# Layer 0's feed-forward: half of its pairs of up tiles as seven block products in place of eight

## The chip, the cores and the metric

The kernel runs on one core of a Trainium2 chip. A core has a matrix engine (TensorE, PE in the profile, with its weight loads as PEld), VectorE (DVE), ScalarE (ACT), GpSimd (POOL) and SyncE (SP), which mostly issues DMAs here. Each engine works through its own list of instructions in order; semaphores between the lists make one wait for another. The metric is the device time of one execution in microseconds (us); lower is better. Times given are medians of several executions; the profile is of one execution.

## The reference

Two blocks of a network follow each other, all in 32-bit floats. The first maps 256 tokens of width 1024 through one gated linear attention layer and a squared-ReLU MLP. The second has two layers over 256 latent and 256 context tokens. Layer 0 mixes by neighbourhood attention, layer 1 by grouped-query attention, and each has a SwiGLU feed-forward (FFN) with a hidden width of 2816. Scale, shift and gate of every norm and residual come from a conditioning vector by one matrix product a layer (`ada`), six rows of 1024 for each layer, for the latent and for the context tokens.

```
def swiglu_ffn(h, w_in, w_out):
    a, g = jnp.split(h @ w_in, 2, axis=-1)
    return (jax.nn.silu(a) * g) @ w_out

def ada_norm(x, g, shift, scale):
    return rms_norm_2(x, g) * (1.0 + scale) + shift
```

In layer 0, latent and context tokens pass through the same FFN weights, so its up product is 512 tokens x 1024 by 1024 x 5632, and its down product 512 x 2816 by 2816 x 1024.

## The kernel before, in words

**Products.** All large products are made in three terms. A weight tile `raw` of 128 x 1024 comes from DRAM (`w_load`, SP). `w_split` turns it into a high part `wh` (a cast on ACT, line 178) and a low part `wl` (a subtraction on DVE, line 179), and the activations are split the same way. `mm3` (lines 193 to 195) adds high x high, low x high and high x low in a PSUM bank. Weight tiles are used in the order of one long list, `UNITS`; `wnext` takes the next and loads and splits some ahead.

**Layer 0's FFN.** The hidden width is 22 tiles of 128; a *pair* is the tile of `a` and the tile of `g` for the same hidden columns. `ffn_up` makes a pair: for each of its two weight tiles eight steps over the input width, three products each, with 512 tokens as moving columns, 48 products of 128x512 in all. `ffn_act` (lines 1109 to 1119) evacuates it: silu on ACT, the product with `g` on DVE (line 1112), a cast on ACT, a subtraction on DVE (line 1119). The first two pairs are made in halves of 256 tokens (`ffn_up_first`). The 22 pairs go in two halves of 11. After each half, `ffn_down0` makes the down product in PSUM banks, which `gated` multiplies by the gate and adds to the residual (lines 1080 and 1081). After the second half the context tokens' down products come first, and the normalising and transposing of the context tokens for layer 1 (`to_T`, lines 232 to 251) is put inside the last call for the latent tokens. The key and value products of layer 1 (`kv_pass`) come next.

**The conditioning steps.** `ada_jobs` makes the rows of `ada` without PE: for eight slices of each row it loads 128 x 1024 numbers (512 KB, SP, line 304, two buffers of tag `ada`) and lets DVE multiply them by the conditioning vector and sum them (line 324, one pass for a *single* step; two for a *double* one, which serves latent and context). After eight steps POOL adds a bias (line 339), and for gate rows PE transposes the result (line 348) so that it can be written to DRAM and fetched again spread over the partitions (`load_gates`). Steps are taken from a generator by `ada_run`. `adaC` has 24 double and 32 single steps; the FFN takes two of them beside each pair and one beside each down tile.

**Order.** A scheduler at build time lays every engine's instructions into one list from the program's dependences and its own estimates, so the program's text sets the order only in part; the lists quoted below are those of the built kernels.

Of the kernel before, what the change touches and what calls it, by code (L numbers as in the profile page):

```python
# [17 lines left out]
P = 128  # L18
# [10 lines left out]
HALF = NFT // 2  # L29
# [7 lines left out]
def _units():  # L37
# [23 lines left out]
    for part in range(2):  # L61
        for f in range(part * HALF, (part + 1) * HALF):
            u += [("f", "ffn_in0", P * f), ("f", "ffn_in0", FH + P * f)]
        dn = [("h", "ffn_out0", part * HALF + f, 512 * h) for h in range(2) for f in range(0, HALF, 2)]
        u += dn if part == 0 else dn + dn
# [18 lines left out]
def net(ctx, tc, x, xt, small, gk_up, gk_b, g_onorm, wst, final_norm, ctx_in, ctx_t, ada, ada_b, cvec,  # L84
# [76 lines left out]
    def w_split(upto):  # L161
        while wpos[1] < min(upto, len(UNITS)):
            i = wpos[1]
            raw = raws.pop(i)
            n = 512 if UNITS[i][0] == "h" and UNITS[i][1] == "ffn_out0" and (UNITS[i][2] % HALF) == HALF - 1 else 1024
# [14 lines left out]

    def wnext(kind):
# [10 lines left out]
    def mm3(o, lh, ll, rh, rl, first, last):  # L192
        T.matmul(o, lhsT=lh, rhs=rh, start=first, stop=False)  # L193
        T.matmul(o, lhsT=ll, rhs=rh, start=False, stop=False)  # L194
        T.matmul(o, lhsT=lh, rhs=rl, start=False, stop=last)  # L195
# [30 lines left out]
    def to_T_steps(xns, dst, t0, scale=None, bias=None):  # L226

        n = P * len(xns)
        for k in range(KD):
# [12 lines left out]
            else:  # L242
                r = t2([n])
# [33 lines left out]
    def mm_h(o, u, j, xp, t, first, last):  # L277
        h, l = u
        c = slice(j * 512, (j + 1) * 512)
        mm3(o, xp[0][:, t * P:(t + 1) * P], xp[1][:, t * P:(t + 1) * P], h[:, c], l[:, c], first, last)  # L280
# [93 lines left out]
    adaC = ada_jobs([(0, 5, True), (1, 0, True), (1, 1, True)] + [(1, v, False) for v in (3, 4, 2, 5)])  # L374
# [726 lines left out]
    fT = new_T2()  # L1101
    o_half(1, 2, hc, 1)
    xn = [normed(t) for t in hc]
    o_half(0, 0, lat, 0)
    o_half(1, 0, lat, 0, lambda: to_T(xn, fT, S, mod(0, 1, 4), mod(0, 1, 3)))
# [16 lines left out]
    def ffn_up(L, src, n):  # L1122
        ps_ = []
        for _ in range(2):
            u = wnext(("f", f"ffn_in{L}"))
            o = bank()
            for k in range(KD):
                mm_f(o[:, :n], u, src, k, 0, n, k == 0, k == KD - 1)
            ps_.append(o)
        return ffn_act(*ps_, n)  # L1130

    def ffn_up_first(src):

        us, os_ = [], []
        for _ in range(4):
            us.append(wnext(("f", "ffn_in0")))
            os_.append(bank())
            for k in range(KD):
                mm_f(os_[-1][:, S:N2], us[-1], src, k, S, S, k == 0, k == KD - 1)
        to_T(xn, src, 0, mod(0, 0, 4), mod(0, 0, 3))  # L1140
        z = []
        for n in range(4):
            for k in range(KD):
                mm_f(os_[n][:, 0:S], us[n], src, k, 0, S, k == 0, k == KD - 1)
# [4 lines left out]
    def ffn_down0(hf, uu, tiles, between=None):  # L1149
        ac = {t: bank() for t in tiles}  # L1150
        for f2 in range(0, HALF, 2):
            u = wnext(("h", "ffn_out0"))
            for j in range(min(2, HALF - f2)):
                f = f2 + j
                for t in tiles:
                    mm_h(ac[t], u, j, uu[f], t, f == 0, f == HALF - 1)
            ada_run(adaC)
            if f2 == 4 and between is not None:
                between()
        for t in tiles:  # L1160
            gated((lat + hc)[t], ac[t], 0, t // 2, 5, hf)
# [19 lines left out]
    for part in range(2):  # L1181
        uu = []
        for f in range(HALF):
            if part == 0 and f < 2:
                uu += ffn_up_first(fT) if f == 0 else []
            else:
                uu.append(ffn_up(0, fT, N2))
            ada_run(adaC, 2)
        if part == 0:
            load_gates(0, 5)  # L1190
            for hf in range(2):
                ffn_down0(hf, uu, (2, 3, 0, 1))
        else:
            for hf in range(2):
                ffn_down0(hf, uu, (2, 3))
            xn = [normed(t) for t in hc]
            ffn_down0(0, uu, (0, 1))
# [3 lines left out]
            ffn_down0(1, uu, (0, 1), lambda: to_T(xn, bT2, S, mod(1, 1, 1), mod(1, 1, 0)))  # L1201
# [310 lines left out]
    load_gates(1, 5)  # L1512
# [186 lines left out]
```

## Time and profile before

| | before |
|---|---|
| median of 3 runs | 1257.45 us (1257.27 to 1258.41) |
| the profiled execution, its own time | 1256.72 us |
| its span in the trace | 1254.9 us |
| PE busy | 1244.0 us, 99% |
| DVE busy | 919.9 us, 73% |
| ACT busy | 688.2 us, 55% |
| ada passes on DVE (line 324) from 570 to 870 us | 80 passes, 96.5 us |
| last ada pass starts at | 802.2 us |

The span is what the trace covers; the execution's own time is 1.8 us longer. Busy times count an engine's arithmetic, not its waits. A row of the timeline gives the start, the duration, the engine, the line of the source, the operation, and what it writes and reads, with buffer numbers left out.

### The profile page before, as it was taken

The page shows a single profiled execution, that of the slowest core. Times are in us where ns is not written, and L with a number is a line of the kernel's source. Part 1 is how long each engine was busy: PE and PEld are TensorE (multiplying, and loading weights), DVE is VectorE, ACT ScalarE, POOL GpSimd, SP SyncE. Part 2 cuts the span into 40 slices and gives each one's busy share as a digit, 9 for nine tenths or more (in the row PEclk, how much of TensorE's full clock was granted, in tenths as well). Part 3 has the DMA queues.
Part 4 walks back from the last instruction along what each step waited for, and adds up shares of the span by engine and source line. Part 5 has one row for each costly group of instructions (what it writes and reads, how often), then busy time and mean ns, then how long its engine had stood idle before and what let it go on. Part 6 is the DMA issues. An engine that isn't in the chain of part 4 may idle for free.

```text
span 1254.9 us, 18667 instructions
## 1 busy us (share of the span) xinstructions
PE 1244.0 (99%) x6872; PEld 1043.2 (83%) x6872; DVE 919.9 (73%) x1638; ACT 688.2 (55%) x1344; POOL 78.7 (6%) x137
## 2 busy tenths in 40 slices
PE   9999999999999999999999999999999999999997
PEld 8888889898888777789888888887888777999997
DVE  6959888697989887777877767633667988655555
ACT  8575655666549888655232222323456897544443
POOL 1010000030100000001000000000003220000000
PEclk9999999999999999999999999999999999999999
DMA  8647687787673333463656877633662324656650
GB/s 304 189 151 237 192 289 268 271 277 246 198 249 111 105 110 118 160 197 118 213 177 206 259 266 249 205 100 102 197 204 76 113 84 131 219 187 185 186 185 34
DMA packets 68507, 231.22 MB, mean 184 GB/s; under 512 B 8048, under 2 KB 8736, under 8 KB 68416
## 3 DMA queue, kind: packets, MB, share of 16 engines
q1 hardware_dynamic: 68128, 229.68, 57.0%
q8 instruction: 54, 0.88, 0.3%
q10 hardware_dynamic: 288, 0.35, 0.1%
q14 instruction: 37, 0.30, 0.1%
HBM read 228.93 MB, written 1.07 MB: 183 GB/s over the span
## 4 chain that ended last, share of the span: by engine, by line
PE 95%; ACT 2%; DVE 1%; issue 1%; DMA 0%; POOL 0%; SPq 0%; POOLq 0%; ACTq 0%
PE b L193 28%; PE b L194 28%; PE b L195 28%; PE b L1000 2%; PE b L1469 1%; PE b L981 1%; PE b L232 1%; PE b L1455 1%; PE b L562 1%; PE b L962 1%; PE b L963 1%; PE b L951 1%; PE b L1436 1%; DVE wl L179 0%; DMA t<-in_xt_dram 0%
## 5 line engine op out<-in xcount | busy, mean ns | idle before, releaser
L178 ACT CAST wh<-raw 128x1024 fp32r<-128x1024 f32 (+1 forms) x308 | 320.7, 1045 | 392.8 <-PE b L194 292.4
L179 DVE TENSOR_TENSOR wl<-raw,wh 128x1024 fp32r<-128x1024 f32 (+1 forms) x308 | 372.5, 1216 | 154.9 <-ACT wh L178 151.9
L193 PE MATMUL b<-t,wh 128*128 128x256 f32 (+1 forms) x1120 | 365.7, 327 | 0.0
L194 PE MATMUL b<-t,wl 128*128 128x256 f32 (+1 forms) x1120 | 365.6, 327 | 0.0
L195 PE MATMUL b<-t,wh 128*128 128x256 f32 (+1 forms) x1120 | 365.3, 327 | 0.0
L193 PE MATMUL b<-wh,t 128*128 128x512 f32 (+1 forms) x748 | 299.2, 402 | 1.2 <-ACT t L250 0.6
L194 PE MATMUL b<-wh,t 128*128 128x512 f32 (+1 forms) x748 | 294.8, 394 | 0.0
L195 PE MATMUL b<-wl,t 128*128 128x512 f32 (+1 forms) x748 | 294.7, 394 | 0.0
L193 PEld LDWEIGHTS b<-t,wh 128*128 128x128 f32 x1120 | 210.7, 188 | 22.2
L194 PEld LDWEIGHTS b<-t,wl 128*128 128x128 f32 x1120 | 210.8, 188 | 21.9
L195 PEld LDWEIGHTS b<-t,wh 128*128 128x128 f32 x1120 | 210.5, 188 | 20.4 <-DVE t L251 0.2
L195 PEld LDWEIGHTS b<-wl,t 128*128 128x128 f32 x748 | 140.4, 188 | 34.2
L193 PEld LDWEIGHTS b<-wh,t 128*128 128x128 f32 x748 | 140.4, 188 | 32.2 <-ACT t L250 1.0
L194 PEld LDWEIGHTS b<-wh,t 128*128 128x128 f32 x748 | 140.8, 188 | 30.1 <-DVE t L251 0.5
L324 DVE CUSTOM_DVE_ANT_0 a<-a,crow 128x1024 f32<-128x1024 f32 x96 | 117.6, 1233 | 28.8 <-DMA a<-in_ada_dram 28.3
L324 DVE CUSTOM_DVE_ANT_0 t<-a,crow 128x1024 bf16<-128x1024 f32 x64 | 78.5, 1237 | 7.3 <-DMA a<-in_ada_dram 7.1
L1112 DVE TENSOR_TENSOR t<-b,t 128x512 f32<-128x512 f32 (+1 forms) x42 | 23.7, 564 | 59.4 <-PE b L195 52.2
L205 POOL TENSOR_TENSOR c<-c,mhalf 128x1 f32<-128x1 f32 x21 | 14.2, 676 | 539.0 <-DVE c L204 538.9
L339 POOL TENSOR_TENSOR mod<-mod,bcol 128x8 f32<-128x8 f32 x20 | 13.4, 671 | 475.1 <-DVE mod L324 472.7
L1118 ACT CAST t<-t 128x512 fp32r<-128x512 f32 (+1 forms) x42 | 21.7, 516 | 28.6 <-DVE t L1112 28.6
L212 ACT ACTIVATE t<-t 128x512 f32<-128x512 f32 x40 | 24.8, 624 | 10.8 <-DVE t L1081 6.4
L1445 ACT ACTIVATE t<-b,c,c 128x512 f32<-128x512 f32 x32 | 26.0, 812 | 3.5 <-POOL c L1443 3.5
(244 smaller groups left out, 1212.6 us busy)
## 6 DMA issues: line engine op xcount, KB each, us to landing
raw<-in_wst_dram SPq DMA_DIRECT2D x310, 512.0 KB, 4.4
a<-in_ada_dram SPq DMA_DIRECT2D x96, 512.0 KB, 4.4
t<-in_rpb_dram SPq DMA_DIRECT2D x16, 256.0 KB, 4.5
t<-row SPq DMA_DIRECT2D x12, 256.0 KB, 5.1
t<-in_ctx_dram SPq DMA_DIRECT2D x8, 256.0 KB, 5.6
t<-in_xt_dram SPq DMA_DIRECT2D x4, 256.0 KB, 5.8
t<-in_x_dram SPq DMA_DIRECT2D x4, 256.0 KB, 6.5
crow<-in_cvec_dram SPq DMA_DIRECT2D x2, 512.0 KB
```

Source lines behind the costliest of these rows:

```text
L178: A.copy(out=h[:, :n], in_=raw[:, :n])
L179: V.tensor_tensor(out=l[:, :n], in0=raw[:, :n], in1=h[:, :n], op=ALU.subtract)
L193: T.matmul(o, lhsT=lh, rhs=rh, start=first, stop=False)
L194: T.matmul(o, lhsT=ll, rhs=rh, start=False, stop=False)
L195: T.matmul(o, lhsT=lh, rhs=rl, start=False, stop=last)
L205: G.tensor_tensor(out=ms[:, 3:4], in0=ms[:, 2:3], in1=mhalf[:, 0:1], op=ALU.pow)
L212: A.activation(out=junk[hf], in_=halves[hf], func=AF.Square, scale=1.0 / 32.0, accum_out=ms[:, hf:hf + 1])
L324: V.tensor_tensor_reduce(out=raw if ci == n_c - 1 else t2([D], BF16), in0=raw, in1=crow[ci], scale=1.0, scalar=0.0, op0=ALU.mult, op1=ALU.add,
L1000: T.matmul(po[e * 64:(e + 1) * 64, cols_], lhsT=v, rhs=probs[(head, "l" if lat_q else "c")][:, c, :], start=(c == 0), stop=(c == n_c - 1))
L1112: V.tensor_tensor(out=a, in0=pg_[:, :n], in1=a, op=ALU.mult)
L1118: A.copy(out=h, in_=a)
L1445: A.activation(out=pl, in_=sl, func=AF.Exp, scale=r, bias=mx[:, 1:2], accum_out=mx[:, 2:3])
```

## The change

- **Four parts for two halves.** The 22 pairs go in parts of 6, 6, 6 and 4. After each part the down product goes on accumulating: `ffn_down0` copies the four banks to SBUF (`dsum`) for one half of the output columns and copies the other half's sums back into the banks (`seed`), and products then accumulate onto them. `ffn_down0_last` does the last part, context first, then latent, with `gated` at its end.
- **Seven block products.** For 11 of the pairs, those listed in `SEVEN`, the pair is taken as a 2 x 2 block product: the two weight tiles by the two halves of the input width, and the two halves of the input by latent and context tokens. Seven products of block sums replace the eight plain ones (`ffn_up7`). Each is 12 products of 128x256, 84 a pair.
- **What the sums need.** `pair_sums` makes the weight sums on DVE and splits three full tiles and a half one, beside the pair before. `token_sums` makes the sums of the tokens once, after pairs 2 to 4, from unsplit copies `fX`. The banks of `ffn_up7` are copied out by ACT and summed by DVE in between (lines 1237 to 1262).
- **Residuals.** The residual tiles are written to DRAM after pair 2 (`put_away`) and read back in the last part (`fetch`).
- **Conditioning steps.** `adaC` has 48 steps (24 double, 24 single). One is taken beside each pair (none beside pair 3) one after the third part and one beside six of the last part's down tiles; what is left is taken in one call, `ada_run(adaC, 100)`, ahead of the last down call. The eight steps of row (1, 5) are a generator of their own, `adaD`, taken beside the first 12 hidden tiles of layer 1's FFN.

Line numbers move: 179 becomes 180, 193 to 195 become 198 to 200, 232 becomes 237, 324 becomes 329, 348 becomes 353, 1080 becomes 1086.

```
-HALF = NFT // 2
+PARTS = ((0, 6), (6, 12), (12, 18), (18, 22))
+SEVEN = (5, 7, 9, 11, 13, 14, 16, 17, 19, 20, 21)
...
-        while wpos[1] < len(UNITS) and wpos[1] - wpos[2] + 1 < cap[0]:
+        while wpos[1] < len(UNITS) and wpos[1] - wpos[2] + 1 < cap[0] and not seven(UNITS[wpos[1]]):
...
-    adaC = ada_jobs([(0, 5, True), (1, 0, True), (1, 1, True)] + [(1, v, False) for v in (3, 4, 2, 5)])
+    adaC = ada_jobs([(0, 5, True), (1, 0, True), (1, 1, True)] + [(1, v, False) for v in (3, 4, 2)])
+    adaD = ada_jobs([(1, 5, False)])
...
+    def ffn_up7(got, conv):
+        wpos[2] += 2
+        r, q, g = [bank()[:, 0:S] for _ in range(3)]
+        c1, c2, c3 = t2([2, S]), t2([2, S]), t2([2, S])
+        H = KD // 2
+
+        def prod(o, n, c, X, first=True):
+            h, l = got[n]
+            for j in range(H):
+                k = slice(c + j * P, c + (j + 1) * P)
+                mm3(o, h[:, k], l[:, k], *X(j), first and j == 0, j == H - 1, not first)
...
+        prod(r, 0, 0, lambda j: a(0, j))
+        A.copy(out=c1[:, 0, :], in_=r)
+        prod(q, 1, 0, lambda j: sT[(3, j)])
+        A.copy(out=c3[:, 0, :], in_=q)
+        run(conv)
+        prod(r, 2, 512, lambda j: sT[(2, j)], False)
+        A.copy(out=c3[:, 1, :], in_=r)
+        prod(g, 0, 512, lambda j: a(0, H + j))
+        got[0] = None
+        V.tensor_tensor(out=c1[:, 0, :], in0=g, in1=c1[:, 0, :], op=ALU.add)
+        A.activation(out=c1[:, 0, :], in_=c1[:, 0, :], func=AF.Silu)
+        run(conv)
+        prod(r, 2, 0, lambda j: sT[(1, j)], False)
+        got[2] = None
+        V.tensor_tensor(out=c2[:, 1, :], in0=r, in1=c3[:, 0, :], op=ALU.add)
+        run(conv)
+        prod(q, 3, 0, lambda j: a(1, H + j), False)
+        V.tensor_tensor(out=c1[:, 1, :], in0=q, in1=c3[:, 1, :], op=ALU.add)
+        A.activation(out=c1[:, 1, :], in_=c1[:, 1, :], func=AF.Silu)
+        V.tensor_tensor(out=c2[:, 1, :], in0=c2[:, 1, :], in1=c1[:, 1, :], op=ALU.mult)
+        run(conv)
+        prod(r, 1, 512, lambda j: sT[(4, j)], False)
...
+    for lo, hi in PARTS:
         uu = []
-        for f in range(HALF):
...
-                uu.append(ffn_up(0, fT, N2))
-            ada_run(adaC, 2)
-        if part == 0:
-            load_gates(0, 5)
...
+            if f != 3:
+                ada_run(adaC)
...
+            fetch(lat, 0)
             xn = [normed(t) for t in hc]
-            ffn_down0(0, uu, (0, 1))
+            ffn_down0_last(0, uu, (0, 1), 1)
+            dsum.clear()
             bT2 = new_T2()
             ada_run(adaC, 100)
             cap[0] = 7
-            ffn_down0(1, uu, (0, 1), lambda: to_T(xn, bT2, S, mod(1, 1, 1), mod(1, 1, 0)))
+            ffn_down0_last(1, uu, (0, 1), 0, lambda: to_T(xn, bT2, S, mod(1, 1, 1), mod(1, 1, 0)))
+            dbank.clear()
             xn = [normed(t) for t in lat]
...
-    load_gates(1, 5)
...
+        if f < 12:
+            ada_run(adaD)
+        if f == 12:
+            load_gates(1, 5)
```

**PE at the end of the FFN.** Before, in PE's list among the last down products of layer 0's FFN: transposes of the normalised context tokens (L232, out of tile `t_8658` and its like), then a down product of the latent tokens (L193, 128x512).

```order
L232 MATMUL b_8909<-cm,t_8658 128x128 [waits DVE_49]
L232 MATMUL b_8909<-cm,t_8667 128x128
L232 MATMUL b_8916<-cm,t_8658 128x128 [waits DVE_49]
L232 MATMUL b_8916<-cm,t_8667 128x128
L232 MATMUL b_8923<-cm,t_8658 128x128 [waits DVE_49]
L232 MATMUL b_8923<-cm,t_8667 128x128
L193 MATMUL b_8801<-wh_8811,t_8114 128x512 [waits Activation_49]
L194 MATMUL b_8801<-wh_8811,t_8115 128x512
```

And now, the same place: the last down products of the FFN (L198 to L200), the transpose of a conditioning row (L353, `mod_9491` is gate row (1, 2)), and the first transposes of the context tokens (L237).

```order
L200 MATMUL b_6843<-wl_9412,t_9105 128x512
L198 MATMUL b_6843<-wh_9411,t_9230 128x512
L199 MATMUL b_6843<-wh_9411,t_9231 128x512
L200 MATMUL b_6843<-wl_9412,t_9230 128x512
L353 MATMUL b_9517<-cm,mod_9491 8x128 [waits Pool_49]
L237 MATMUL b_9582<-cm,t_9370 128x128
L237 MATMUL b_9582<-cm,t_9379 128x128
L237 MATMUL b_9589<-cm,t_9370 128x128
```

The context's transposes stood ahead of down products that were still to come; now they stand behind all of them, and behind a transpose that waits for POOL's bias on row (1, 2), the last row of `adaC`.

**DVE at the end of `adaC`.** Before, in DVE's list: the last three ada steps (L324, each a pass and the read-out of its sum) among the evacuations of a pair (L1112, L1119) and splits of weight tiles (L179).

```order
L324 ISA a_8351,mod_8195<-a_8351,crow_87 128x1024 [waits DMAHW4_49,DVE_49]
L324 ISA mod_8195 128x1
L1112 TENSOR_TENSOR t_7883<-b_7858,t_7883 128x512 [waits PE_49,Activation_49]
L179 TENSOR_TENSOR wl_8008<-raw_7899,wh_8007 128x1024 [waits Activation_49]
L1119 TENSOR_TENSOR t_7887<-t_7883,t_7886 128x512 [waits Activation_49]
L324 ISA a_8354,mod_8195<-a_8354,crow_87 128x1024 [waits DMAHW6_49]
L324 ISA mod_8195 128x1
L324 ISA a_8426,mod_8195<-a_8426,crow_87 128x1024 [waits DMAHW7_49]
L324 ISA mod_8195 128x1
L179 TENSOR_TENSOR wl_8052<-raw_7930,wh_8051 128x1024 [waits PE_49,Activation_49]
```

And now, beginning at the last two splits before the run of ada steps; the second of them, `wl_9567`, takes a buffer that the FFN's last down product reads.

```order
L180 TENSOR_TENSOR wl_9549<-raw_9528,wh_9548 128x1024 [waits DMAHW2_49,PE_49,Activation_49]
L180 TENSOR_TENSOR wl_9567<-raw_9534,wh_9566 128x1024 [waits PE_49,Activation_49]
L329 ISA a_9455,mod_9327<-a_9455,crow_87 128x1024 [waits DMAHW1_49,DVE_49]
L329 ISA mod_9327 128x1
L329 ISA a_9458,mod_9327<-a_9458,crow_87 128x1024 [waits DMAHW2_49,DVE_49]
L329 ISA mod_9327 128x1
L329 ISA a_9461,mod_9466<-a_9461,crow_87 128x1024 [waits DMAHW5_49,DVE_49]
L329 ISA mod_9466 128x1
```

The ada steps that ended among pairs now end in a run of 18 behind those splits. The first evacuation of a context transpose (L253) comes behind the run, and the eight steps of `adaD` stand between the evacuations that follow and ahead of the latent tokens' last gate and norm passes.

**PE inside a pair.** Now, in a pair in sevens: the end of the third block product into bank `b_1795`, four products of the sixth into bank `b_1796`, and the fifth, which accumulates in `b_1795` again.

```order
L200 MATMUL b_1795_9122<-t_1432_6711,wh_1784_9069 128x256
L198 MATMUL b_1796_9123<-t_1245_5760,w_1786_9089 128x256 [waits Activation_49]
L199 MATMUL b_1796_9123<-t_1245_5760,w_1786_9089 128x256
L200 MATMUL b_1796_9123<-t_1246_5761,w_1786_9089 128x256
L198 MATMUL b_1796_9123<-t_1247_5762,w_1786_9089 128x256
L198 MATMUL b_1795_9122<-t_1387_6514,wh_1784_9069 128x256 [waits Activation_49]
L199 MATMUL b_1795_9122<-t_1387_6514,wl_1785_9070 128x256
```

A plain pair had two banks and no copy within it; here the fifth block product waits for ACT's copy of the third with four products between.

More of the change, by code (lines that the diff above doesn't have):

```diff
@@ L179, in w_split, with seven @@
                 V.tensor_tensor(out=l[:, :n], in0=raw[:, :n], in1=h[:, :n], op=ALU.subtract)
+    def seven(u):
+        return u[1] == "ffn_in0" and u[2] % FH // P in SEVEN
     def wnext(kind):
@@ L1101, in net @@
     fT = new_T2()
+    fX = [t2([2, S]) for _ in range(KD)]
     o_half(1, 2, hc, 1)
```

189 lines of the change are left out of this document (153 added, 36 removed).

## The prediction

> **What bounds the kernel now.** I read the page first: its busy table, the granted clock over the span and the chain of work that ended last.
>
> ```profile
> span 1254.9 us, 18667 instructions
> ...
> PE 1244.0 (99%) x6872; PEld 1043.2 (83%) x6872; DVE 919.9 (73%) x1638; ACT 688.2 (55%) x1344; POOL 78.7 (6%) x137
> ...
> PEclk9999999999999999999999999999999999999999
> ...
> PE 95%; ACT 2%; DVE 1%; issue 1%; DMA 0%; POOL 0%; SPq 0%; POOLq 0%; ACTq 0%
> ```
>
> TensorE (PE) is busy 99% of the span at full clock and makes 95% of the chain, so only 10.9 us are not PE's. A change pays by what it takes from PE's stream, and costs by every wait that it puts into it. The second view is the table of busy time by stretch (columns: us, then PE, PEld, DVE, ACT and POOL busy with instruction counts, granted clock, DMA share, GB/s). From 575 to past 900 us the kernel works on layer 0's feed-forward (FFN).
>
> ```profile
> 575.00:715.00 140.00, 140.00 (x634) 114.07 (x634) 106.09 (x158) 41.39 (x52) 3.96 (x6) 1.00 0.66 208
> 715.00:780.00 65.00, 65.00 (x280) 52.28 (x279) 48.17 (x74) 14.91 (x18) 1.36 (x3) 1.00 0.77 252
> 780.00:803.00 23.00, 23.00 (x100) 18.50 (x99) 16.05 (x23) 6.71 (x9) 1.08 (x1) 1.00 0.80 262
> 803.00:870.00 67.00, 67.00 (x288) 53.77 (x288) 23.91 (x27) 18.55 (x26) 1.12 (x1) 1.00 0.33 104
> 870.00:900.00 30.00, 30.00 (x131) 24.06 (x130) 16.02 (x17) 12.02 (x14) 0.00 (x0) 1.00 0.60 177
> ```
>
> PE never waits here. VectorE (DVE) is busy 76% up to 715, 74% up to 780, and only 36% from 803 to 870. The step at 803 is where the conditioning steps (ada) end: each is a DMA of 512 KB and one or two passes of DVE over it. So before the change they all lie beside up products, and nothing of them is left at the end of the FFN, where PE waits for whatever DVE still owes.
>
> The third view is PE's timeline, 128x512 first (first and last of 50 in a row), then 128x256 (first and last of 41 in a row).
>
> ```profile
> 640.48 0.39 PE L194 MATMUL b<-t,wl 128*128 128x512 f32 x1
> ...
> 651.96 0.39 PE L195 MATMUL b<-t,wh 128*128 128x512 f32 x1
> ```
>
> ```profile
> 564.15 0.28 PE L193 MATMUL b<-t,wh 128*128 128x256 f32 x1
> ...
> 568.90 0.28 PE L194 MATMUL b<-t,wl 128*128 128x256 f32 x1
> ```
>
> The pace is 11.48/49 = 0.2343 us for 512 columns and 4.75/40 = 0.1188 us for 256. A product of half the width costs half; the 0.39 and 0.28 us in the second column are latencies that overlap.
>
> **Term 1, products saved.** A plain pair is 48 products of 512, 11.25 us. A pair in seven block products is 84 of 256, 9.98 us. Eleven pairs: 11 x 1.27 = **-14.0 us**. The down products stay at 528 of 512 columns.
>
> **Term 2, waits inside the eleven pairs.** First DVE's timeline from 784 us (the last bracket is idle time and what ended it; L324 is an ada pass, L179 a split of a weight tile).
>
> ```profile
> 784.50 1.23 DVE L324 CUSTOM_DVE_ANT_0 a<-a,crow 128x1024 f32<-128x1024 f32 x1 [1.18 <-DMA a<-in_ada_dram]
> 785.65 0.08 DVE L324 DVE_READ_ACCUMULATOR2_ANT mod<- 128x1 f32 x1
> 785.65 0.69 DVE L1112 TENSOR_TENSOR t<-b,t 128x512 f32<-128x512 f32 x1
> 786.25 1.22 DVE L179 TENSOR_TENSOR wl<-raw,wh 128x1024 fp32r<-128x1024 f32 x1
> 787.39 0.69 DVE L1119 TENSOR_TENSOR t<-t,t 128x512 fp32r<-128x512 f32 x1
> ...
> 790.10 1.23 DVE L324 CUSTOM_DVE_ANT_0 a<-a,crow 128x1024 f32<-128x1024 f32 x1 [0.88 <-DMA a<-in_ada_dram]
> ...
> 796.64 1.22 DVE L324 CUSTOM_DVE_ANT_0 a<-a,crow 128x1024 f32<-128x1024 f32 x1 [1.32 <-DMA a<-in_ada_dram]
> ...
> 802.25 1.23 DVE L324 CUSTOM_DVE_ANT_0 a<-a,crow 128x1024 f32<-128x1024 f32 x1 [0.90 <-DMA a<-in_ada_dram]
> ```
>
> The next rows are group means (before the bar: busy us, mean ns).
>
> ```profile
> L179 DVE TENSOR_TENSOR wl<-raw,wh 128x1024 fp32r<-128x1024 f32 x302 | 368.4, 1227 | 154.9 <-ACT wh L178 151.9 <-DMA raw<-in_wst_dram 0.8
> ...
> L1080 DVE TENSOR_TENSOR t<-b,t 128x512 f32<-128x512 f32 x29 | 19.3, 685 | 4.2 <-PE b L195 4.2
> ...
> L251 DVE TENSOR_TENSOR t<-t,t 128x256 fp32r<-128x256 f32 x40 | 15.5, 421 | 3.5 <-ACT t L250 3.1
> ...
> L219 DVE TENSOR_SCALAR t<-t,c 128x512 f32<-128x512 f32 x22 | 9.8, 486 | 6.8 <-POOL c L205 6.8
> ```
>
> ```profile
> L1462 ACT COPY t<-b 128x256 f32<-128x256 f32 x64 | 21.7, 403 | 2.8 <-PE b L1455 2.8
> ```
>
> ```profile
> L339 POOL TENSOR_TENSOR mod<-mod,bcol 128x8 f32<-128x8 f32 x20 | 13.4, 671 | 475.1 <-DVE mod L324 472.7 <-DVE mod L341 2.3
> ```
>
> The fifth block product goes on accumulating in a bank that ACT (ScalarE) has first to copy out, and PE has four small products (0.48 us) in between. It needs 0.28 us to the end of the product before and 0.40 us for the copy, so about 0.3 us with hand-offs is open. The last block product waits in the same way for a DVE add of 0.42 us with eight products (0.95 us) in between; DVE may just then be in a split or an ada pass of 1.2 us, so 0 to 1.0 us is open. DVE's own load is near the limit too: for a pair in sevens it makes three splits (1.227 each) and five operations on 512 columns (0.685 each), 7.1 us, evacuates by 5 x 0.421 + 0.685 = 2.8 us, and has an ada step of one or two passes, 1.15 us each (784.50 to 785.65): 11 to 12 us against PE's 9.98, with neighbours overlapping by some 0.08 each. Bounds 0.3 to 1.3 us a pair; I take 0.5, nearer the row of the copy, which always applies: **+5.5 us** (3 to 14).
>
> **Term 3, the end of the FFN.** The changed kernel runs one ada step for each pair where it ran two, and starts with 48 steps here. At the end of the FFN 18 single steps stand on DVE in one run, behind a split that waits for PE's last product of the FFN. PE's next instruction is the transpose of a conditioning row that needs the last of them; the sixteen transposes of the context tokens and the key/value products stand behind it in PE's queue. So PE stands still from its last down product until the run is over. The price of a step comes from the timeline above, where the steps of before wait longest.
>
> ```profile
> DMA to landing us min/median/max: 3.5/4.4/6.5
> ```
>
> A pass takes DVE 1.15 us (784.50 to 785.65) and a split 1.14 (786.25 to 787.39). But there are two buffers, and a load can start only when the step two before has been read. The rows are every second step, that is one buffer: read at 785.73, used again at 790.10, 4.37 us later; then 5.31 (791.33 to 796.64) and 4.38 (797.87 to 802.25). With the pass of 1.23 a buffer comes round in 5.6 to 6.5 us, a step every 2.8 to 3.3 us, while the bracket shows that DVE waited for the DMA. In the run nothing else uses the queue, so I take 2.84.
>
> - Step 3a, DVE arrives late. From the start of the last pair in sevens to the run, PE has 10.0 + 96 x 0.2343 = 32.5 us of products. DVE has 12 splits (13.7), four double and six single ada steps (14 passes, 16.1), 12 gate passes by 0.685 (8.2), four norm passes by 0.486 (1.9) and the pair's evacuation (2.8): 42.7 us, and some 1.1 us of DMA wait (the brackets) for each of the six single steps, 49.3. PE is held up on the way too, since the last down products start from sums that are copied into the banks only after a gate pass. **+16.8 us** (10 to 22).
> - Step 3b, the run: two steps whose data is there, 2.3 us, and 16 x 2.84 = 45.4: **+47.7 us** (42 to 55).
> - Step 3c, behind it POOL's bias (0.67 us), the transposes and the first evacuations until a product can start: **+1.5 us** (0.5 to 3). Before, this lay inside the last down products.
> - Step 3d: the eight steps of the last conditioning row, meant for layer 1's FFN, stand right behind the run, between the evacuations on which the key/value products wait and ahead of the last gate and norm passes of the latent tokens: 8 x 2.84 = 22.7 us, against 11.25 us of key/value products. **+11 us** (4 to 15).
>
> The Trainium skill bears on two of these. For 3b, "DMA: Bandwidth & Descriptors" (Latency and other measured facts; Measured (HBM→SBUF)) gives some 2 us of fixed cost and 341 GB/s for 1 MB; an estimate from it is 3.5 us for one load, 2.3 us a step and 37 us for the 16, which would make the whole some 12 us shorter. Its 3.5 is the minimum of the landing row here, and the waits of 4.4 to 5.3 decide. For the gap as a whole, "TensorE: Matmul & The Clock Gate" (What's actually happening) says that an idle window of 3.4 us halves PE's clock until it has been busy about as long: an estimate of 1.7 us more. PEclk is 9 in all slices here, and no PE gap of that length stands in this trace to show it.
>
> Moves that cost nothing: putting the residual away (eight stores on ACT's queue) and fetching it (eight loads on SP) stand beside up and down products, and DVE is first to need them; if a fetch is late it lengthens 3a by its landing. The token sums stand behind pairs of 11.25 us. Fewer weight tiles (300 for 310) only unload SP.
>
> **Sum.** -14.0 + 5.5 + 16.8 + 47.7 + 1.5 + 11 = +68.5 us on the profiled execution's own 1256.7 us (span 1254.9 and 1.8 around it): 1325.2. The median of the runs is 1257.45, 0.7 above the profiled one, so about **1325 us**, slower by 5%.
>
> **The rivals.** About 0.2% (2.5 us) is what a measurement of this kernel can tell from no change.
>
> - *The run at DVE's pace.* If loads in a run with an empty queue kept up, a step would cost 1.15: 18 x 1.15 = 20.7, DVE's lateness 10, the last row hidden but for 2: -14 + 5.5 + 10 + 20.7 + 1.5 + 2 = +26, **1283 us**. For it: the brackets above are 0.9 to 1.3 us, no more than a pass. Against it: there other work lay between two steps, and the DMA was late still. Chance 0.10.
> - *DVE sets the pace of the sevens.* If each seven costs DVE 11.8 us and PE follows, term 2 is some 1.8 us a pair: 20 instead of 5.5, **1340 us**. For it: the count of 11 to 12 against 9.98. Against: plain pairs between sevens give 11.25 us of PE for less DVE work. Chance 0.07.
> - *The other side: the run is hidden.* Were DVE far enough ahead to finish the 18 steps before PE's last down product, only terms 1 and 2 would stay: **1249 us**. DVE has 36% of load in 803 to 870 before, which speaks for room; it would have to gain 17 + 48 us there. Against: the split ahead of the run waits for that last product itself, so the run can't start earlier; even at 1.15 a step PE would idle 20 us, more than term 1. It decides if the executed order is not the one listed. Chance 0.03.
>
> The forecast has the rest, 0.80. Its own bounds, not all at the same end, are 1300 to 1342; with the next rival's 1283 left out and the sevens' 1340 in, the range is 1295 to 1345. Slower by over 0.2%: 0.80 + 0.10 + 0.07 = 0.97; the other side gives 0.02 faster and 0.01 within 0.2%.
>
> **What would show it.** In the changed profile, PE's busy slices should show one hole at the end of layer 0's FFN, of 50 to 65 us, with DVE in ada passes 2.8 us apart and idle for the DMA between them, and PE's first transpose released by POOL. The key/value stretch behind it should show PE about half busy. Eleven stretches of pairs should have 84 products at 0.119 us with gaps of about 0.5 us in all. PE busy in the whole should fall by about 14 us. The prediction is wrong if no hole stands there, if the passes of the run follow each other at 1.2 us, or if the gaps in the pairs are over 1.3 us each.

## The result, and the profile after

The changed kernel takes 1322.59 us (median of 4 runs, 1320.50 to 1324.60), the kernel before 1257.93 beside it (4 runs, 1257.27 to 1258.86): a ratio of 1.0513, 95% interval 1.0495 to 1.0531. The profiled execution took 1322.47 us, 65.8 us more than the 1256.7 of before.

The page of the changed kernel: busy time, PE in 40 slices of 33 us, the granted clock in the same slices, and the chain that ended last.

```profile
span 1320.7 us, 19700 instructions
...
PE 1240.2 (94%) x7268; PEld 1059.0 (80%) x7268; DVE 973.0 (74%) x1746; ACT 743.3 (56%) x1456; POOL 75.0 (6%) x137
...
PE   9999999999999999999999999997118999999997
...
PEclk9999999999999999999999999998558999999999
...
PE 87%; DMA 5%; DVE 3%; ACT 2%; issue 1%; POOL 0%; SPq 0%; POOLq 0%; DVEq 0%; ACTq 0%
```

Where every slice of PE but the last was a 9, there is one hole now. The chain has 5% of DMA in it, where it had 0%. PEclk is the second thing to see: it is down around the hole. Which wait made the hole says the table of PE's waits (us in total, times, longest).

```profile
PE b L353 <- POOL mod L344: 56.6, 1, 56.6
PE b L198 <- ACT b L1287: 6.6, 1, 6.6
PE b L237 <- DVE t L224: 4.0, 2, 3.3
PE b L198 <- DVE t L253: 2.1, 1, 2.1
```

POOL is the last link only; what stood before it is on DVE's timeline through the hole (start, length, and in brackets idle time and what ended it).

```profile
935.88 1.22 DVE L329 CUSTOM_DVE_ANT_0 a<-a,crow 128x1024 f32<-128x1024 f32 x1
...
938.18 1.23 DVE L329 CUSTOM_DVE_ANT_0 a<-a,crow 128x1024 f32<-128x1024 f32 x1 [1.08 <-DMA a<-in_ada_dram]
...
952.95 1.23 DVE L329 CUSTOM_DVE_ANT_0 a<-a,crow 128x1024 f32<-128x1024 f32 x1 [1.52 <-DMA a<-in_ada_dram]
...
955.75 1.23 DVE L329 CUSTOM_DVE_ANT_0 a<-a,crow 128x1024 f32<-128x1024 f32 x1 [1.57 <-DMA a<-in_ada_dram]
...
983.52 1.23 DVE L329 CUSTOM_DVE_ANT_0 a<-a,crow 128x1024 f32<-128x1024 f32 x1 [1.75 <-DMA a<-in_ada_dram]
```

This is the run of 18 ada steps, from 935.88 to 984.76. Each pass but the first waits for its load, by 0.30 to 3.27 us: from the first start to the last it is 47.64 us for 17 steps, 2.80 us each, of which the pass is 1.15. And PE's timeline on both sides of the hole:

```profile
914.28 0.79 PE L198 MATMUL b<-wh,t 128*128 128x512 f32 x1 [6.62 <-ACT b L1287]
914.88 0.63 PE L199 MATMUL b<-wh,t 128*128 128x512 f32 x1
915.30 0.63 PE L200 MATMUL b<-wl,t 128*128 128x512 f32 x1
...
920.36 0.40 PE L200 MATMUL b<-wl,t 128*128 128x512 f32 x1
...
928.05 0.39 PE L200 MATMUL b<-wl,t 128*128 128x512 f32 x1
985.09 0.38 PE L353 MATMUL b<-cm,mod 128*8 128x128 f32 x1 [56.65 <-POOL mod L344]
985.26 3.51 PE L237 MATMUL b<-cm,t 128*128 128x128 f32 x16
990.88 0.50 PE L198 MATMUL b<-wh,t 128*128 128x512 f32 x1 [2.11 <-DVE t L253]
...
1007.23 0.85 PE L237 MATMUL b<-cm,t 128*128 128x128 f32 x6 [3.34 <-DVE t L224]
1008.75 2.25 PE L237 MATMUL b<-cm,t 128*128 128x128 f32 x10 [0.67 <-DVE t L224]
```

The 56.65 us are not all of it. Ahead of the hole PE waits 6.62 us for a seed (the sums copied back into a bank), and behind it, from 914.88 on, the products start 0.43 us apart where the pace was 0.2343. The table by stretch (PE, PEld, DVE, ACT, POOL, granted clock, DMA share, GB/s) says why.

```profile
907.00:914.20 7.20, 0.67 (x3) 0.19 (x1) 6.39 (x10) 1.60 (x2) 0.20 (x1) 0.71 1.02 399
914.20:920.40 6.20, 6.12 (x15) 4.79 (x16) 6.20 (x14) 2.19 (x4) 0.58 (x1) 0.51 0.77 244
920.40:929.00 8.60, 8.04 (x35) 6.15 (x33) 7.87 (x14) 5.82 (x13) 1.19 (x2) 1.00 0.94 337
...
985.00:989.00 4.00, 3.68 (x17) 3.39 (x17) 2.22 (x5) 1.53 (x4) 0.03 (x1) 0.56 0.63 152
989.00:992.30 3.30, 1.42 (x5) 1.15 (x6) 2.83 (x6) 1.28 (x3) 0.00 (x0) 0.95 0.73 218
992.30:995.30 3.00, 3.00 (x9) 2.31 (x8) 2.27 (x5) 1.28 (x3) 0.00 (x0) 0.50 0.61 203
```

The granted clock falls during the wait and stays at half for 6 us of work behind it. DVE is busy 6.39 of the 7.20 us around the wait. Behind the hole the clock is at half again for the transposes (0.56), back at full (0.95), and at half once more from 992.30 (0.50).

### The profile page after: what moved, and what is told of

Its sections match the earlier page's. It is cut to its first block, busy times and chain, and to the rows that moved or that the text cites. A ratio compares the mean times of both kernels' runs of the same rounds, so it can differ in the third digit from the quotient of the medians.

```text
span 1320.7 us, 19700 instructions
## 1 busy us (share of the span) xinstructions
PE 1240.2 (94%) x7268; PEld 1059.0 (80%) x7268; DVE 973.0 (74%) x1746; ACT 743.3 (56%) x1456; POOL 75.0 (6%) x137
## 4 chain that ended last, share of the span: by engine, by line
PE 87%; DMA 5%; DVE 3%; ACT 2%; issue 1%; POOL 0%; SPq 0%; POOLq 0%; DVEq 0%; ACTq 0%
PE b L198 26%; PE b L199 25%; PE b L200 25%; DMA a<-in_ada_dram 5%; PE b L1006 2%; DVE a L329 1%; PE b L1657 1%; PE b L987 1%; PE b L1643 1%; PE b L237 1%; DVE wl L180 1%; PE b L568 1%; PE b L968 1%; PE b L969 1%; PE b L957 0%
## 5 line engine op out<-in xcount | busy, mean ns | idle before, releaser
L180 DVE TENSOR_TENSOR wl<-raw,wh 128x1024 fp32r<-128x1024 f32 x276 | 336.0, 1226 | 151.2 <-ACT wh L179 126.2
L179 ACT CAST wh<-raw 128x1024 fp32r<-128x1024 f32 x276 | 289.2, 1053 | 222.1 <-PE b L199 159.1
L198 PE MATMUL b<-t,wh 128*128 128x256 f32 (+1 forms) x1208 | 371.1, 308 | 0.0
L199 PE MATMUL b<-t,wl 128*128 128x256 f32 (+1 forms) x1208 | 370.0, 307 | 0.0
L200 PE MATMUL b<-t,wh 128*128 128x256 f32 (+1 forms) x1208 | 369.3, 307 | 0.0
L198 PE MATMUL b<-wh,t 128*128 128x512 f32 (+1 forms) x748 | 300.0, 403 | 9.9 <-ACT b L1287 6.6
L200 PE MATMUL b<-wl,t 128*128 128x512 f32 (+1 forms) x748 | 296.4, 397 | 0.0
L198 PEld LDWEIGHTS b<-t,wh 128*128 128x128 f32 x1208 | 227.3, 188 | 16.8 <-DVE t L1250 1.3
L199 PEld LDWEIGHTS b<-t,wl 128*128 128x128 f32 x1208 | 227.6, 188 | 14.0
L200 PEld LDWEIGHTS b<-t,wh 128*128 128x128 f32 x1208 | 227.0, 188 | 12.5 <-DVE t L1179 0.2
L198 PEld LDWEIGHTS b<-wh,t 128*128 128x128 f32 x748 | 141.6, 190 | 41.5 <-ACT b L1287 7.1
L200 PEld LDWEIGHTS b<-wl,t 128*128 128x128 f32 x748 | 141.7, 189 | 33.8
L1197 DVE TENSOR_TENSOR wl<-raw,wh 128x1024 fp32r<-128x1024 f32 x33 | 40.3, 1221 | 44.9 <-ACT wh L1196 30.9
L1196 ACT CAST wh<-raw 128x1024 fp32r<-128x1024 f32 x33 | 34.7, 1051 | 55.5 <-PE b L199 30.3
L353 PE MATMUL b<-cm,mod 128*8 128x128 f32 x6 | 1.4, 289 | 56.6 <-POOL mod L344 56.6
L353 PEld LDWEIGHTS b<-cm,mod 128*8 128x8 f32 x6 | 0.5, 84 | 57.5 <-POOL mod L344 57.1
```

Of the source, the lines that this page charges most:

```text
L179: A.copy(out=h[:, :n], in_=raw[:, :n])
L180: V.tensor_tensor(out=l[:, :n], in0=raw[:, :n], in1=h[:, :n], op=ALU.subtract)
L198: T.matmul(o, lhsT=lh, rhs=rh, start=first, stop=False, skip_group_check=onto)
L199: T.matmul(o, lhsT=ll, rhs=rh, start=False, stop=False, skip_group_check=onto)
L200: T.matmul(o, lhsT=lh, rhs=rl, start=False, stop=last, skip_group_check=onto)
L1196: A.copy(out=h, in_=r)
```

## The experiments

Before them stood one question that the trace alone doesn't answer: is the loss the run of ada steps and nothing else, so that a kernel without the run keeps the 14 us of the sevens? The theory said yes. The rivals: the sevens themselves load DVE so much that they cost what they save; or the run is paced by DVE and not by its loads. All ratios below are to the kernel before, measured on the same chip.

### Two steps beside each pair

```
-                ada_run(adaC)
+                ada_run(adaC, 2)
```

> Two conditioning steps beside each pair in place of one, all else as in the change; the run of 18 steps and the steps of the last row then stand among the pairs. Theory (the loss is the run at the end, and the pairs in sevens themselves save 13.25 us): the hole of 56.8 us goes, the key/value stretch gets back some 7 us, what stood behind the run some 4 us, and most of the 9.8 us lost in the last down products: 1247 us (1242 to 1256), below the kernel before. Rival (DVE is at its limit in the sevens, so more steps there stop PE): gaps of 1 us and more a pair, 1256 to 1275 us.

Measured: 1256.49 us (10 runs), ratio 0.999 (0.998 to 0.9999). The hole and the 6.6-us seed wait are gone, so the steps that had been left over to the end made both. But 1247 was expected, and most of the gain is missing. PE's timeline at the end of the FFN:

```profile
922.09 1.47 PE L237 MATMUL b<-cm,t 128*128 128x128 f32 x12
927.35 0.44 PE L237 MATMUL b<-cm,t 128*128 128x128 f32 x2 [3.79 <-DVE t L253]
...
929.60 0.80 PE L198 MATMUL b<-wh,t 128*128 128x512 f32 x1 [0.66 <-DVE t L253]
930.20 0.63 PE L199 MATMUL b<-wh,t 128*128 128x512 f32 x1
```

The sixteen transposes of the context and their evacuations stand behind the last down product now. Before the change they stood among down products; now nothing covers them: 7.5 us from 922.09 to 929.60, of which about 1.7 are the transposes' own. The products behind them start at half clock (0.43 us apart; the granted clock from 929 to 934 is 0.50), some 2 us more. Gaps in the pairs add 3.4. So the run hid a second loss, which comes from the order of the last part: the transposes behind its last product.

### The gate row first, and no last row

Two kernels ask what in the hole belongs to the order of the rows. The first puts row (1, 2), on which L353 waits, ahead of the other two; the second drops `adaD` and gives its place to a row that is there.

```
-    adaC = ada_jobs([...] + [(1, v, False) for v in (3, 4, 2)])
+    adaC = ada_jobs([...] + [(1, v, False) for v in (2, 3, 4)])
```

> The three single rows in the order 2, 3, 4 in place of 3, 4, 2, so that the gate row, whose transpose stands in PE's queue, is not the last; just as many steps are left over at the end. In the list of instructions two steps, not 18, then stand ahead of the first evacuation, and 11 more between the evacuations up to the latent tokens' transposes. Theory (PE waits for whatever steps stand ahead of the next evacuation, 2.84 us each): 13 steps count in place of 18 and 8, the hole shrinks to some 12 us and the key/value stretch is paced by steps: 1290 us (1280 to 1300). Rival (only the gate row's transpose holds PE): 1260 us. Rival (the left-over steps cost the same wherever they stand): 1315 to 1322 us.

Measured: 1290.24 us (2 runs), ratio 1.026 (1.024 to 1.0281), as expected. PE's waits:

```profile
PE b L353 <- POOL mod L344: 12.4, 1, 12.4
PE b L237 <- DVE t L224: 8.5, 4, 4.2
PE b L198 <- ACT b L1287: 6.1, 1, 6.1
```

The hole shrinks from 56.6 to 12.4 us and the rest of the steps comes between the evacuations of the key/value stretch, where PE waits in small pieces. Half of the loss (32.3 of 64.7 us) hung on which row comes last.

```
-        if f < 12:
-            ada_run(adaD)
         if f == 12:
+            grows[(1, 0, 5)] = grows[(1, 0, 2)]
             load_gates(1, 5)
```

> The eight steps of row (1, 5) are left out (layer 1's FFN takes the other gate row in their place, so that part of the computation is changed); the run of 18 stays. Theory: only the key/value stretch gets shorter, by the 5 to 7 us that the steps between its evacuations cost: 1317 us (1314 to 1320), hole 56 to 57 us. Rival (those steps lie beside the products): 1322 us.

Measured: 1315.09 us (2 runs), ratio 1.0458 (1.0437 to 1.0479): 7.5 us less than with `adaD`, and the hole as it was (57.6). So `adaD` costs some 7 us behind the hole.

### The run without its loads

On top of the last one: the 16 steps of rows (1, 4) and (1, 2) read a tile that has been loaded already.

```
                 if (L, v) in ((1, 4), (1, 2)):
                     loaded[n] = held[0]
                     return
```

> As the kernel without the last row, and 16 of the 18 steps of the run multiply a tile that is there already in place of loading one (so these rows are wrong). The instructions on DVE and their order stay. Theory (the run goes at the pace of two buffers and a load of 4.4 us): a step takes 1.2 us in place of 2.84, the hole shrinks by 16 x 1.65 = 26 us to about 30, 1290 us (1285 to 1296). Rival (the step's own time on DVE, its read-out and hand-offs set the pace): no change, 1315 us.

Measured: 1288.87 us (2 runs), ratio 1.0249 (1.0229 to 1.027). DVE's timeline in the run:

```profile
939.91 1.22 DVE L333 CUSTOM_DVE_ANT_0 a<-a,crow 128x1024 f32<-128x1024 f32 x1
...
941.18 1.22 DVE L333 CUSTOM_DVE_ANT_0 a<-a,crow 128x1024 f32<-128x1024 f32 x1
```

A step takes 1.27 us, and PE's wait for the row's transpose (L353, here L357) falls to 32.3. That is the price of waiting for the loads: 26.2 us of the time, 16 steps by 1.5 us being 24.5. That two buffers set it, and not the rate of the DMA, is argued and not shown: 512 KB in 2.80 us are 187 GB/s, and the table by stretch has 399 GB/s from 907 to 914.2, but no run had a third buffer. The forecast's first rival, a run at DVE's pace, would have been near this.

### All pairs plain

```
-SEVEN = (5, 7, 9, 11, 13, 14, 16, 17, 19, 20, 21)
+SEVEN = ()
```

> No pair in sevens: all 22 pairs plain, with the four parts, the residuals in DRAM and the conditioning steps as in the change. DVE has some 50 us less to do; in its list 17 steps stand in a run behind the last split. Theory (the gain of 13.25 us in the sevens is real, but half of what DVE was late at the run, some 17 us, came from them): PE's last down product comes 13 us later by the products and 10 us earlier by the stall that goes, DVE reaches the run right behind it, and the run is one step shorter: 1316 us (1308 to 1328), not above the change in spite of 13 us more products. Rival (the two parts of the change simply add): 1322.6 + 13.25 = 1336 us.

Measured: 1332.40 us (2 runs), ratio 1.0596 (1.0575 to 1.0617). The theory's 1316 failed; the rival, by which the parts simply add, is nearer with 1336. I had taken DVE's lateness at the run for a consequence of the sevens. It isn't: here PE's own work would end some 13.25 us later than in the changed kernel (918.9, below, plus 14.0 less 0.75 of gaps, is 932.1), and DVE starts the run late by as much as there.

```profile
949.34 1.23 DVE L329 CUSTOM_DVE_ANT_0 a<-a,crow 128x1024 f32<-128x1024 f32 x1
```

949.34 less 932.1 is 17.2 us, where the changed kernel has 17.0. With two steps beside each pair none were left beside the last part, and there was no such lateness. So it goes with the ada steps beside the last down tiles, whatever the pairs are, as far as these two runs tell. The sevens are worth 9.8 us in this frame, that is with all else the same (1332.40 less 1322.59; two runs that lie 2.4 us apart and four that lie 4.1 apart, so by a few us either way).

### A version that keeps the gain

From here the question was where the 14 us go once the run is gone. `between` (the transposes of the context) is called at the first down tile of the last call, so that down products follow it again:

```
-            if f2 == 2 and between is not None:
+            if f2 == 0 and between is not None:
```

With two steps a pair:

> As two steps a pair, and the context's transposes put behind the first, not the second, of the last call's two down tiles. Theory (the 9 us that were missing there are 3.4 us of waits in the pairs, 5.9 us of transposes and evacuations that nothing covers at the end of the FFN, and 2.8 us of halved clock behind that gap): the last two go, 1248 us (1246 to 1253). Rival (the transposes wait for the context's last gate and norm passes, and the wait only moves forward): 1256 us.

Measured: 1254.87 us (10 runs), ratio 0.9983 (0.9974 to 0.9992): faster than both kernels, by 2.6 us instead of the 9 expected. PE's timeline at the end of the FFN:

```profile
925.65 0.44 PE L237 MATMUL b<-cm,t 128*128 128x128 f32 x2 [1.81 <-DVE t L253]
...
928.00 0.76 PE L198 MATMUL b<-wh,t 128*128 128x512 f32 x1 [0.80 <-DVE t L253]
928.57 0.63 PE L199 MATMUL b<-wh,t 128*128 128x512 f32 x1
928.99 0.63 PE L200 MATMUL b<-wl,t 128*128 128x512 f32 x1
```

The longest wait falls from 3.79 to 1.81 us, but a last part of 4 pairs still doesn't cover the evacuations, the products behind them start at half pace again, and gaps of some 3 us stay in the pairs. Next, one step a pair, and one beside each down tile of the first three parts (`ada_run(adaC)` in the loop of `ffn_down0`):

> As the change, with the early transposes, one step beside each pair, and one beside each down tile of the first three parts too, where DVE has little to do. Theory: the waits in the pairs go back to the 0.8 us of the change, and nothing is left over at the end: 1245 us (1243 to 1250). Rival (the end of the FFN is bound by DVE whatever is placed where): 1252 us or more.

Measured: 1256.31 us (10 runs), ratio 0.9993 (0.9983 to 1.0002). No better: a wait of 2.6 us for ACT (L1237) has come into the pairs, and 2.4 us for L253 stay at the end. The same with `SEVEN = ()`:

> As the one before with all pairs plain: what the sevens alone are worth when the conditioning steps are out of the way. Theory: 13.25 us of products more: 1258 us (1255 to 1262). Rival (PE's gain in the sevens is lost to DVE): the same as the one before within 3 us.

Measured: 1262.54 us (4 runs), ratio 1.0041 (1.0026 to 1.0055). The sevens are worth 6.2 us in this frame. Then the last part made longer, six pairs instead of four, to cover its end, with two steps a pair:

```
-PARTS = ((0, 6), (6, 12), (12, 18), (18, 22))
-SEVEN = (5, 7, 9, 11, 13, 14, 16, 17, 19, 20, 21)
+PARTS = ((0, 4), (4, 10), (10, 16), (16, 22))
+SEVEN = (5, 7, 9, 11, 13, 14, 15, 17, 19, 20, 21)
```

> As two steps a pair with the early transposes, and parts of 4, 6, 6 and 6 pairs (pair 15 in sevens in place of 16), so that the last down calls have three tiles each and the context's transposes have two of them behind, not one. Theory (of the 14 us of products saved, some 3 us go into waits in the pairs and 7 us into the end of the FFN, where the context's gates, norms, transposes and evacuations are one chain on DVE with too few down products to cover it): 5 of the 7 us come back, 1250 us (1248 to 1253). Rival (the chain takes as long wherever it stands): 1254 to 1257 us.

Measured: 1258.18 us (11 runs), ratio 1.0009 (1.0000 to 1.0019), where 1250 was expected. The end is covered (about 2 us of waits are left), but the gaps in the pairs have grown to some 11 us. DVE's timeline shows one of them being made:

```profile
659.52 1.22 DVE L329 CUSTOM_DVE_ANT_0 t<-a,crow 128x1024 bf16<-128x1024 f32 x1
...
660.67 1.22 DVE L329 CUSTOM_DVE_ANT_0 t<-a,crow 128x1024 bf16<-128x1024 f32 x1
...
661.81 1.22 DVE L329 CUSTOM_DVE_ANT_0 a<-a,crow 128x1024 f32<-128x1024 f32 x1
...
662.96 1.22 DVE L329 CUSTOM_DVE_ANT_0 a<-a,crow 128x1024 f32<-128x1024 f32 x1
...
664.11 0.68 DVE L1119 TENSOR_TENSOR t<-b,t 128x512 f32<-128x512 f32 x1
```

Two double steps are four passes, 4.6 us, and they stand ahead of L1119, which empties a bank that PE wants; PE stands 1.70 us for it. DVE's mean load says nothing of this; what stands in its list ahead of the next evacuation does. The same frame with `SEVEN = ()`:

> As the one before with all pairs plain. Theory: the end of the FFN is covered here too, so this is the kernel before in another frame, 1257 to 1260 us, and the sevens' worth is the difference, 8 to 10 us (14 less the waits in the pairs). Rival (the four parts, the copies and the residuals in DRAM cost by themselves): 1262 us or more.

Measured: 1259.72 us (10 runs), ratio 1.002 (1.0011 to 1.0029), as expected. Here the sevens are worth 1.5 us, hardly more than these runs tell apart (the two intervals overlap). Now one step a pair and one a down tile in these parts, with the first loads of `adaD` held back until layer 1's FFN:

```
+            ada_run(adaC)
...
-            if f != 3:
-                ada_run(adaC)
+            ada_run(adaC)
```

> The longer last part with early transposes; one conditioning step beside each pair and each down tile in place of two beside each pair, and the last row's steps held back to layer 1's FFN by a copy that their first loads wait for. In the list of DVE at most two passes then stand ahead of an evacuation in the sevens, where there were four to six. Theory (the sevens lose what they gain when evacuations stand behind several passes of conditioning steps on DVE: 11 us of waits in 11 pairs with two steps a pair, under 1 us with one): waits in the pairs of 1 to 4 us, end of the FFN covered: 1249 us (1246 to 1253), below all before. Rival (DVE's whole load decides, not what stands ahead of what): 1256 us or more.

Measured: 1257.73 us (11 runs), ratio 1.0001 (0.9992 to 1.001), again not the 1249 expected. One place carries most of it; PE's timeline, then the table by stretch (the clock is the third number from the end):

```profile
643.30 0.27 PE L357 MATMUL b<-cm,mod 128*8 128x128 f32 x1
646.94 0.58 PE L198 MATMUL b<-t,wh 128*128 128x256 f32 x1 [3.37 <-ACT t L1182]
...
648.90 0.41 PE L200 MATMUL b<-t,wh 128*128 128x256 f32 x1
649.12 0.41 PE L198 MATMUL b<-t,wh 128*128 128x256 f32 x1
```

```profile
640.00:660.00 20.00, 15.66 (x95) 14.30 (x94) 15.56 (x27) 8.75 (x16) 0.00 (x0) 0.83 0.25 72
```

The token sums (L1182) come 3.37 us late, and the clock is halved behind that: 0.83 over 20 us, so 20 x 0.17 = 3.4 us more. One wait costs 6.8 us. The changed kernel leaves out the step beside pair 3, and this edit had put it back; I took DVE's passes there for the cause. (DVE's timeline has no ada pass there: none starts between 639 and 647.9.) The last kernel deals the steps by place: none beside pairs 3 and 4, where the token sums are made, none beside a seven that another seven follows, two beside a seven that a plain pair follows.

```
-            ada_run(adaC)
+            ada_run(adaC, {0: 2, 3: 0, 4: 0, 5: 2, 7: 2, 9: 2, 11: 2, 13: 0, 14: 0,
+                           15: 2, 17: 2, 19: 0, 20: 0, 21: 0}.get(f, 1))
```

> e13_spread with the steps of adaC dealt by place: none beside pairs 3 and 4, where the token sums are made, none beside a seven that another seven follows, two beside a seven that a plain pair follows, one beside the other pairs; the steps beside the down tiles stay. Theory (what is left of the sevens' gain is eaten by DVE passes that stand ahead of the next eviction): the wait of 3.4 us behind the token sums and the half clock behind it (about 3.4 us more) go, and no other wait of TensorE in the pairs passes 1 us: 1249 to 1252 us. Rival (the waits only move to where two steps stand now, four passes in a row ahead of an eviction): a wait of 2 to 4 us elsewhere in the pairs, and 1256 to 1260 us.

Measured: 1250.20 us (5 runs, 1248.58 to 1250.76), ratio 0.9943 (0.9929 to 0.9956), as expected and the best version of the study. Its page, PE's two longest waits from 600 to 940 us, and PE's timeline where the token sums are waited for:

```profile
span 1246.8 us, 19701 instructions
...
PE 1233.1 (99%) x7268; PEld 1053.1 (84%) x7268; DVE 971.9 (78%) x1748; ACT 744.5 (60%) x1458; POOL 79.5 (6%) x139
```

```profile
PE b L237 <- DVE t L224: 0.7, 1, 0.7
PE b L198 <- DVE t L1124: 0.6, 1, 0.6
```

```profile
642.76 0.39 PE L198 MATMUL b<-t,wh 128*128 128x512 f32 x1
...
646.41 0.39 PE L198 MATMUL b<-t,wh 128*128 128x256 f32 x1
```

The wait is gone, but not for the reason given. The last line of the token sums first starts on DVE 6.76 us behind the pair's first product (645.61 less 638.85), and with the spread steps it was 6.77 (646.15 less 639.38): DVE gained nothing. What is new is PE's list: from 642.76 it holds 15 products 128x512 of the next, plain pair, where the kernel with the spread steps had only the transpose of a gate row and then stood. So the scheduler's order filled the wait. That the steps' places brought this order about follows from the edit, which has nothing else; by which of its rules it did was not tried. This one place was worth 6.8 us, and the whole step from the spread steps to here is 7.5 (1257.73 less 1250.20): most of it came in a way that was not planned.

The last kernel issues the same 7268 products as the changed kernel, and DVE is as busy in all (971.9 us, 973.0 there); only the places of the ada steps, of the parts and of the context's transposes differ, and the time by 72 us. Of the 14.0 us, 8.1 come through (spans 1254.9 and 1246.8). Counted from start to start of PE's products against their pace, 3.0 us of the rest are gaps in the pairs and 2.4 at the end of the FFN; the last 0.5 is not located. No run has this frame with plain pairs, so what the sevens alone are worth here is not measured.

## Why the prediction was right

The forecast was 1325 us (1295 to 1345), slower, and the kernel takes 1322.59. Step by step, from the changed trace:

- **Term 1, -14.0.** PE's busy time was to fall by about 14 us and falls by 3.8 only (1244.0 to 1240.2). Products at half clock count as busy for longer, some 7.5 us (below); the other 2.7 are not accounted for. It falls by 10.9 in the last experiment, which has the same products and no half clock in the FFN. The -14.0 itself stands only as far as the sum closes.
- **Term 2, +5.5 expected, 0.75 measured:** five gaps of about 0.15 us. The copy of 0.40 us, which I took as always open, is nearly always covered by the four products in between. This term was mis-sized in the kernel as it was changed. Its mechanism (an evacuation that stands behind 1.2-us passes) is real: with steps at other places the gaps were 3 to 11 us.
- **3a, +16.8 expected, 17.0 measured.** From the end of the 6.62-us wait PE has 48 products to 928.28; at 0.2343 they end 11.25 us after 907.66, at 918.9, and the run begins at 935.88. PE itself loses 9.4 of these 17.0 on the way, 6.62 to the seed and 2.8 to the half clock behind it. The step named the seed wait, not the clock. That the size came out is in part luck. In the 49.5 us from 886.4 (32.5 us of products ahead of 918.9) to the run, DVE is busy for 45.1 us, where 42.7 were counted (it makes 14 splits, not 12), and waits 1.4 for its loads, where 6.6 were; another 3.0 us it idles for PE and others. Two wrong sizes nearly cancel.
- **3b, +47.7 expected, 48.9 measured,** 2.80 us a step against 2.84. The estimate from the Trainium skill, "DMA: Bandwidth & Descriptors" (Latency and other measured facts), was 2.3 us a step and 12 us less in all; the measurement decides, and two buffers whose turns came from the trace gave the better price. The run without its loads shows by experiment that 1.5 of the 2.8 us are the loads'.
- **3c, +1.5 expected, 4.4 measured** (984.76 to 990.88, less the 1.7 us that the transposes took before): under-sized. The sixteen transposes took 3.51 us at half clock (985.26 to 988.77), and the first product waited 2.11 us more for an evacuation.
- **3d, +11 expected, 6.9 measured** (the key/value stretch takes 19.8 us, from 990.88 to 1010.65, for 12.9 before): over-sized; leaving `adaD` out gave back 7.5. The rest of its 22 us lay beside PE's products; what PE felt is 3.34 and 0.67 us on L224, and half clock. The stretch was to be about half busy; PE is busy 15.8 of the 19.8 us.

The sum by these values is -14.0 + 0.75 + 17.0 + 48.9 + 4.4 + 6.9 = 64.0, against 65.8 of span. Of the 1.8 us left, 0.9 are four products at half clock behind 1010.65, where the last term ends (1.83 us for 0.94); the other 0.9 builds up over the rest of the kernel, and why was not looked into. So the mechanism held, its two large terms to about an us, and terms 2 and 3d (8.9 us too much) offset 3c and the rest. That the whole came within 3 us is luck to that extent.

**The clock.** No term held it. The Trainium skill, "TensorE: Matmul & The Clock Gate" (What's actually happening), gave an estimate of 1.7 us. The trace agrees with the rule that idle time of that length halves the clock, but around the hole the clock was halved four times, and once behind a wait of 2.11 us only. It cost 2.8 us behind the seed wait (14 products in 6.08 us), 1.6 in the context's transposes (3.51 for 1.91 before), 1.35 in the key/value stretch (7 products in 2.99), and behind the 3.34-us wait some 0.8 in the latent tokens' transposes (eight of them 0.21 us apart, for 0.11 before) and the 0.9 at 1010.65: some 7.5 us in all.

**Which of the rivals' reasons held.** The run at DVE's pace: no, a step took 2.80 us, and 1.27 only where nothing was loaded. The run hidden: no, PE's last product ends at 928.4 and the splits ahead of the run start at 933.6. DVE setting the pace of the sevens: not here, with gaps of 0.75 us in all; in the longer last part with two steps a pair the gaps in the pairs came to 11, and DVE's passes stood ahead of the one that is shown. My reading after the result, that the sevens made DVE late, fell with the plain pairs.

## What to carry to other kernels

Work that an in-order engine does in the background has two prices, and its share of busy time shows neither: what stands in its list ahead of the next evacuation, and what is left when the cover ends, which then runs at the pace of its buffers (2.8 us a step here, for 1.15 of work). So when a stage is made shorter, count the background steps that had lain under it, and deal them out by place. Then look at what the new order did: here the version dealt by place was the best one, but most of its gain over the spread steps came from what PE's list held at the token sums, and DVE's chain there was no faster. A gain on the busiest engine is only kept as far as the chains beside it stay covered: the same eleven pairs in sevens, 14 us of products, were worth 9.8, 6.2 and 1.5 us in three frames.

## What the hardware showed that was not expected

- The clock fell twice around one hole. The sixteen transposes right behind the 56.65 us ran at half pace (3.51 us, granted clock 0.56 from 985 to 989). The first five products behind them were near full pace (from 991.22 three start 0.23 us apart; 0.95), and from 992.30 to 995.29 products were 0.43 apart again (0.50), with no wait ahead of them but the 2.11 us before 990.88.
- One long wait isn't needed. With two steps a pair and early transposes no wait is longer than 1.81 us, yet three waits with a few transposes between (925.65 to 928.00) had products at 0.43 us behind them. What share of idle time it takes no run here measures.
- The clock can cost as much as the wait: a wait of 3.37 us in the spread steps cost another 3.4 us of clock, and one of 6.62 us cost 2.8.
